# A chunked RWKV-7 scan on one core: small products of the two array halves issued in turn

## The chip, the core and the metric

The kernel runs on one core of a Trainium2 chip. The core has a matrix engine (PE, TensorE), which multiplies a stationary operand (`lhsT`, loaded by a weight load, PEld) with a moving operand (`rhs`) and writes to PSUM; a vector engine (DVE), a scalar engine (ACT) and GpSimd (POOL), which do the elementwise work; and SyncE (SP) and others, which issue DMAs. Each engine executes its own instructions in the order in which they stand. The metric is the device time of one execution in microseconds.

## The reference, cut to what matters

Two layers of a streaming encoder (256 tokens, width 2048, float32): attention and a feed-forward block, then RWKV-7 time mixing and a feed-forward block. The change is in the time mixing, a recurrence over tokens with a 64x64 state for each of 32 heads:

```
def step(state, inp):
    rt, wt, kt, vt, kkt, at = inp
    sa = einsum('bhvk,bhk->bhv', state, -kkt)
    state = state * wt + sa[..., None] * (kkt * at) + vt[..., None] * kt
    yt = einsum('bhvk,bhk->bhv', state, rt)
    return state, yt
_, y = lax.scan(step, state0, xs)          # then a norm per head, a gate, and out @ wo
```

## The kernel before

All large products split a float32 operand into a high and a low part and take three matmuls (L216 to L218, moving operand 512 wide; L236 to L238, 256 wide). I call these the large matmuls; DVE and ACT make their weight halves `whi` and `wlo` (L111, L112) from what the DMA queue of SP brings.

The scan does not step through tokens. Tokens go in 4 chunks of 64 and heads in 4 groups of 8 (`g`). Within a chunk the recurrence becomes small float32 products, each of them two passes of the matrix engine (a weight load and a matmul apiece), on a part of the 128x128 array: the rows by the partitions of the operands, the columns by the partitions of the output.

- `scan_operands` (L1110), for each of 8 panels: 16 products of 64x64, 8 on rows 0 to 63 and columns 0 to 63, then 8 on rows and columns 64 to 127, all into one PSUM bank (`ps_d`). This lies beside the projection `rwk`.
- `scan_pre` (L1169), for each group: for each of 8 heads 4 products of 64 rows by 128 columns; even heads use rows 0 to 63, odd heads rows 64 to 127. DVE masks each head's bank (L1172). In group 0 two heads go in one step (banks `ps_d` and `ps_c`), in the others one head (`ps_c`).
- `scan_chain`, for each group: the inverse of a triangular matrix is put together by 32x32 products (L1229, L1238, two halves of 16 each). Then chunk by chunk `c`: `within` (L1254, 8 products of 64x64) into `wps`; `carried` (L1265) adds 4 products with the state `SB` to it, and 4 more go to the output bank `yps` on the other half of the columns; ACT copies `wps` to `W` (L1270); 8 products with the inverse (L1281); ACT copies them to `VU` (L1283); the state's update (L1292, 2 x 4 products, one column half after the other), added to the decayed state by DVE (L1297, L1299); and the outputs (L1301, 8 products on column half `tb`). After every second chunk a head norm starts.

The chain is a generator that is advanced between the large matmuls of the projections `rwv` and `rwo` (`tick`); a scheduler in the framework then puts each engine's instructions in a fixed order, which differs somewhat from the order written. `ps(role)` takes PSUM banks in rotation: three for `mm`, two for `a`, one each for `b`, `c`, `d`.

Of the kernel before, what the change touches and what calls it, by code (L numbers as in the profile page):

```python
# [10 lines left out]
F32 = mybir.dt.float32  # L11
# [3 lines left out]
ALU = mybir.AluOpType  # L15
# [5 lines left out]
P = 128  # L21
# [13 lines left out]
class Kern:  # L35
# [1008 lines left out]
    def scan_operands(self, g, q, tmp, rq, kq):  # L1044

        nc, V_ = self.nc, self.vec
# [31 lines left out]
        for src, dst in ((sq, pn), (rk, pb)):  # L1078
            for t in range(2):
                for i in range(2):  # L1080
                    nc.tensor.matmul(dst[:, t, :], lhsT=src[:, i, t * P:(t + 1) * P], rhs=self.ind[:, i, :],
                                     start=i == 0, stop=i == 1)
# [20 lines left out]
        yield 4  # L1103

        ps = self.ps("d").rearrange("p (i c t) -> p i c t", i=2, c=4)
        for e in range(2):
            x = slice(64 * e, 64 * e + 64)
            for i in range(2):
                for c in range(4):
                    nc.tensor.matmul(ps[x, i, c, :], lhsT=kb[x, 2 * i + c // 2, 1 + c % 2, :], rhs=ar[x, 4 * i + c, 0, :],  # L1110
                                     start=True, stop=True)
        ms = tmp.tile([P, 8, 64], F32, name="ms", tag="ms")
# [31 lines left out]
    @staticmethod  # L1144
    def hx(h):

        return (h // 4) * 4 + (h % 2) * 2 + (h % 4) // 2

    def scan_pre(self, g, ld, sp):

        nc = self.nc
        KB, AR = [], []
        for q in range(2):
            kb = ld.tile([P, 4, 4, 64], F32, name="kb2", tag="KB", bufs=2)
            ar = ld.tile([P, 8, 2, 64], F32, name="ar2", tag="AR", bufs=4)
            (nc.scalar if g else nc.sync).dma_start(kb, self.kbd[2 * g + q])
            (nc.scalar if g else nc.sync).dma_start(ar, self.ard[2 * g + q])
            KB.append(kb.rearrange("p (i b) (e x) t -> p i (b e) (x t)", i=2, e=2))
            AR.append(ar.rearrange("p (i c) s t -> p i c s t", i=2))
            if g == 0:  # L1160
                yield 5 - q
        if g:
            yield 3
        QT = []
        for h in range(8):
            q, i, x = h // 4, (h % 4) // 2, slice(64 * (h % 2), 64 * (h % 2) + 64)
            ps = self.ps("c" if g or h % 2 else "d").rearrange("p (c x) -> p c x", c=4)
            for c in range(4):
                nc.tensor.matmul(ps[:, c, :], lhsT=KB[q][x, i, c, :], rhs=AR[q][x, i, c].rearrange("p s t -> p (s t)"),  # L1169
                                 start=True, stop=True)  # L1170
            qt = sp.tile([P, 4, 128], F32, name="qt", tag="QT", bufs=16)
            nc.vector.tensor_tensor(qt, ps, self.tri.unsqueeze(1).to_broadcast([P, 4, 128]), op=ALU.mult)  # L1172
            QT.append(qt)
            if g or h % 2:
                yield 0

        for q in range(2):
            x = KB[q].rearrange("p i c x -> p (i c) x")
            pl = self.PL[g][:, 2 * q:2 * q + 2, :].rearrange("p i c -> p (i c)")
            (nc.gpsimd if g > 1 else nc.vector).tensor_tensor(x, x, pl.unsqueeze(2).to_broadcast([P, 8, 128]), op=ALU.mult)  # L1180
        yield 0
        return KB, AR, QT

    def scan_chain(self, g, sp, pre, v, norm, done):
        nc, a = self.nc, self.a
        KB, AR, QT = pre

        aside = nc.gpsimd if g else nc.vector

        def bB(c):  # L1190
            return 64 * (1 - c % 2)

        def bK(c):
            return 64 * (c % 2)
# [4 lines left out]
        VU = sp.tile([P, 4, 512], F32, name="VU", tag="VU")  # L1199
        for par in range(2):  # L1200
            b = 64 * (1 - par)
# [3 lines left out]
            for blk in (1, 0):  # L1205
                dst = TP[b + 32 * blk:b + 32 * blk + 32].rearrange("s h a i -> s (h a) i")[:, :, 32 * blk:32 * blk + 32]
# [6 lines left out]
        for pr_ in range(4):  # L1213
            ps = self.ps("dc"[pr_ % 2])
# [7 lines left out]
        done.add(("kbt", g))  # L1222
        hx = self.hx
        ps1 = self.ps("mm").rearrange("p (h a i) -> p h a i", h=8, a=2)
        for par in range(2):
            b = 64 * (1 - par)
            for h in range(8):
                for ap_ in range(2):
                    nc.tensor.matmul(ps1[b + 32:b + 64, hx(h), ap_, :], lhsT=QT[h][b:b + 32, 2 * ap_ + par, 32:64],  # L1229
                                     rhs=T1[b:b + 32, hx(h), ap_, :], start=True, stop=True)  # L1230
            nc.scalar.copy(T1[b + 32:b + 64], ps1[b + 32:b + 64])
        yield 0
        ps2 = self.ps("mm").rearrange("p (h a i) -> p h a i", h=8, a=2)
        for par in range(2):
            b = 64 * (1 - par)
            for h in range(8):
                for ap_ in range(2):
                    nc.tensor.matmul(ps2[b:b + 32, h, ap_, :], lhsT=T1[b + 32:b + 64, h, ap_, :],  # L1238
                                     rhs=TP[b + 32:b + 64, h, ap_, 32:64], start=True, stop=True)
            nc.scalar.copy(TP[b:b + 32, :, :, 32:64], ps2[b:b + 32])  # L1240


        W = sp.tile([P, 512], F32, name="W", tag="W")

        SB = sp.tile([P, 4, 128], F32, name="SB", tag="SB")
        SD = sp.tile([P, 4, 64], F32, name="SD", tag="SD")
        nc.gpsimd.memset(SB, 0.0)
        wps, yps = {}, None

        def within(c):  # L1250

            wps[c] = self.ps("mm")[bB(c):bB(c) + 64, :]
            for h in range(8):
                nc.tensor.matmul(wps[c][:, h * 64:(h + 1) * 64], lhsT=QT[h][bK(c):bK(c) + 64, c, 0:64],  # L1254
                                 rhs=VU[bK(c):bK(c) + 64, c, h * 64:(h + 1) * 64], start=h == 0, stop=c == 0 and h == 7)

        within(0)
        for c in range(4):
            t, b, tb = c // 2, bB(c), 64 * (c % 2)
            if c % 2 == 0:  # L1260
                yps = self.ps("b")

            def carried(dst, s):
                for pr_ in range(4):
                    nc.tensor.matmul(dst[:, pr_ * P:(pr_ + 1) * P], lhsT=AR[pr_ // 2][:, pr_ % 2, c, s, :],  # L1265
                                     rhs=SB[:, pr_, :], start=s == 1 and pr_ == 0, stop=s == 0 and pr_ == 3)

            if c:
                carried(wps[c], 0)
            nc.scalar.copy(W[b:b + 64, :], wps[c])  # L1270
            if c:
                carried(yps[tb:tb + 64, :], 1)
                if c < 3:
                    for e in range(2):
                        x = slice(64 * e, 64 * e + 64)
                        aside.tensor_tensor(SD[x], SB[x, :, x], self.PL[g][x, :, c].unsqueeze(2).to_broadcast([64, 4, 64]),
                                            op=ALU.mult)
            yield 0
            pu = self.ps("mm")
            for h in range(8):  # L1280
                nc.tensor.matmul(pu[b:b + 64, h * 64:(h + 1) * 64], lhsT=TP[b:b + 64, hx(h), t, :],  # L1281
                                 rhs=W[b:b + 64, h * 64:(h + 1) * 64], start=True, stop=True)
            nc.scalar.copy(VU[b:b + 64, c, :], pu[b:b + 64, :])  # L1283
            if c < 3:
                within(c + 1)
            yield 0
            if c < 3:
                ps = self.ps("mm")[:, :256].rearrange("p (r x) -> p r x", r=4)
                for e in range(2):
                    x = slice(64 * e, 64 * e + 64)  # L1290
                    for pr_ in range(4):
                        nc.tensor.matmul(ps[x, pr_, :], lhsT=KBT[pr_][:, c, x],  # L1292
                                         rhs=VU[:, c, (2 * pr_ + e) * 64:(2 * pr_ + e + 1) * 64], start=True, stop=True)
                for e in range(2):
                    x = slice(64 * e, 64 * e + 64)
                    if c:
                        nc.vector.tensor_tensor(SB[x, :, x], ps[x], SD[x], op=ALU.add)  # L1297
                    else:
                        nc.vector.tensor_copy(SB[x, :, x], ps[x])  # L1299
            for h in range(8):  # L1300
                nc.tensor.matmul(yps[tb:tb + 64, h * 64:(h + 1) * 64], lhsT=QT[h][:, c, 64:128],  # L1301
                                 rhs=VU[:, c, h * 64:(h + 1) * 64], start=c == 0 and h == 0, stop=h == 7)
            if c % 2:
                norm(g, t, yps, v)
            yield 0

# [192 lines left out]
```

## Time and profile before

| | us |
|---|---|
| median of 3 runs | 2492.48 (2490.84 to 2494.36) |
| the profiled execution, its own time | 2493.24 |
| its span, first to last instruction | 2491.5 |

The small products of the scan lie between about 1320 and 1717 us of the span. In the listings a matmul's time runs from its start to its modelled end, and matmuls overlap, so the time that a burst costs is read from its first start to the first start of what follows.

### The profile page before, as it was taken

What the parts mean: (1) busy time and instruction counts of PE and PEld (TensorE: products, weight loads), DVE (VectorE), ACT (ScalarE), POOL (GpSimd) and SP (SyncE); (2) the same over time, 40 slices, a digit from 0 to 9 for tenths busy, and PEclk for the clock granted to TensorE, in tenths of its full rate; (3) what the DMA queues carried; (4) which work ended last, traced back from release to release, by engine and by line L of the source; (5) the groups of instructions that cost most, each with busy time, mean ns of one, the idle gap of its engine ahead of it and who ended that gap; (6) DMA issues with size and microseconds to landing.
All of it is one profiled execution on the core that took longest, in us unless ns stands there. A gap on an engine that the chain in (4) does not pass through costs nothing.

```text
span 2491.5 us, 42348 instructions
## 1 busy us (share of the span) xinstructions
PE 2437.7 (98%) x17128; PEld 2214.8 (89%) x17128; DVE 1595.8 (64%) x2498; ACT 1161.6 (47%) x1669; POOL 205.6 (8%) x234
## 2 busy tenths in 40 slices
PE   8999999999999999997999999999999999999997
PEld 8998889989989989986899988888998998998986
DVE  6667978645656646669478965557864555655655
ACT  5435646444444434455556544444544443443443
POOL 1000000000000000014301252211000000000001
PEclk9999999999999999998999999999999999999999
DMA  8665455555555555553456754324555555555554
GB/s 280 209 198 180 140 177 176 188 190 192 187 193 187 189 197 187 191 181 119 154 176 221 255 194 131 108 92 154 177 195 193 189 190 190 187 191 194 187 192 139
DMA packets 140852, 453.01 MB, mean 182 GB/s; under 512 B 27536, under 2 KB 27792, under 8 KB 140656
## 3 DMA queue, kind: packets, MB, share of 16 engines
q1 hardware_dynamic: 120176, 424.46, 51.4%
q0 software_dynamic: 5568, 16.52, 1.8%
q10 hardware_dynamic: 14912, 9.32, 1.2%
q8 instruction: 134, 2.20, 0.3%
q14 instruction: 62, 0.51, 0.1%
HBM read 433.99 MB, written 15.20 MB: 180 GB/s over the span
## 4 chain that ended last, share of the span: by engine, by line
PE 92%; DVE 4%; issue 1%; DMA 1%; ACT 1%; POOL 0%; SPq 0%; DVEq 0%; ACTq 0%
PE ps_mm L236 8%; PE ps_mm L237 7%; PE ps_mm L238 7%; PE ps_mm L218 7%; PE ps_mm L216 7%; PE ps_mm L217 7%; PE ps_a L216 7%; PE ps_a L217 6%; PE ps_a L218 6%; PE ps_a L238 6%; PE ps_a L236 6%; PE ps_a L237 6%; PE ps_c L1169 1%; DVE wlo L112 1%; PE ps_mm L1254 1%
## 5 line engine op out<-in xcount | busy, mean ns | idle before, releaser
L112 DVE TENSOR_TENSOR wlo<-raw,whi 128x1024 fp32r<-128x1024 f32 (+1 forms) x766 | 937.6, 1229 | 621.6 <-ACT whi L111 604.1
L111 ACT CAST whi<-raw 128x1024 fp32r<-128x1024 f32 (+1 forms) x776 | 809.7, 1047 | 681.1 <-PE ps_mm L218 221.0
L236 PE MATMUL ps_mm<-fxh,whi 128*128 128x256 f32 x1024 | 287.7, 281 | 0.0
L237 PE MATMUL ps_mm<-fxl,whi 128*128 128x256 f32 x1024 | 287.3, 281 | 0.0
L236 PE MATMUL ps_a<-fxh,whi 128*128 128x256 f32 x1024 | 286.9, 280 | 0.0
L237 PE MATMUL ps_a<-fxl,whi 128*128 128x256 f32 x1024 | 286.9, 280 | 0.0
L238 PE MATMUL ps_a<-fxh,wlo 128*128 128x256 f32 x1024 | 286.9, 280 | 0.0
L238 PE MATMUL ps_mm<-fxh,wlo 128*128 128x256 f32 x1024 | 286.9, 280 | 0.0
L217 PE MATMUL ps_mm<-wlo,uh 128*128 128x512 f32 (+1 forms) x544 | 208.2, 383 | 0.0
L216 PE MATMUL ps_mm<-whi,uh 128*128 128x512 f32 (+1 forms) x544 | 208.2, 383 | 0.0
L218 PE MATMUL ps_mm<-whi,ul 128*128 128x512 f32 (+1 forms) x544 | 208.2, 383 | 0.0
L217 PE MATMUL ps_a<-wlo,uh 128*128 128x512 f32 (+1 forms) x512 | 196.0, 383 | 0.0
L238 PEld LDWEIGHTS ps_a<-fxh,wlo 128*128 128x128 f32 x1024 | 195.9, 191 | 0.0
L238 PEld LDWEIGHTS ps_mm<-fxh,wlo 128*128 128x128 f32 x1024 | 195.9, 191 | 0.0
L218 PE MATMUL ps_a<-whi,ul 128*128 128x512 f32 (+1 forms) x512 | 195.7, 382 | 0.0
L216 PE MATMUL ps_a<-whi,uh 128*128 128x512 f32 (+1 forms) x512 | 195.5, 382 | 0.0
L236 PEld LDWEIGHTS ps_mm<-fxh,whi 128*128 128x128 f32 x1024 | 192.2, 188 | 0.6 <-DVE r L630 0.2
L237 PEld LDWEIGHTS ps_mm<-fxl,whi 128*128 128x128 f32 x1024 | 192.3, 188 | 0.3
L237 PEld LDWEIGHTS ps_a<-fxl,whi 128*128 128x128 f32 x1024 | 192.2, 188 | 0.0
L236 PEld LDWEIGHTS ps_a<-fxh,whi 128*128 128x128 f32 x1024 | 192.2, 188 | 0.0
L632 ACT CAST uh<-r 128x256 fp32r<-128x256 f32 x128 | 51.9, 406 | 271.1 <-DVE r L631 271.1
L237 PE MATMUL ps_mm<-ml,whi 128*128 128x256 f32 x416 | 118.0, 284 | 6.7 <-DVE ml L807 6.7
(404 smaller groups left out, 4796.5 us busy)
## 6 DMA issues: line engine op xcount, KB each, us to landing
raw<-in_ffn SPq DMA_DIRECT2D x512, 512.0 KB, 4.3
raw<-in_wk SPq DMA_DIRECT2D x32, 512.0 KB, 4.6
raw<-in_wv SPq DMA_DIRECT2D x32, 512.0 KB, 4.1
raw<-in_wo SPq DMA_DIRECT2D x32, 512.0 KB, 4.1
raw<-in_rwr SPq DMA_DIRECT2D x32, 512.0 KB, 4.6
raw<-in_rwk SPq DMA_DIRECT2D x32, 512.0 KB, 4.3
raw<-in_rwv SPq DMA_DIRECT2D x32, 512.0 KB, 5.1
raw<-in_rwo SPq DMA_DIRECT2D x32, 512.0 KB, 4.3
```

Source lines behind the costliest of these rows:

```text
L111: self.nc.scalar.copy(hi[:, x], src[:, x])
L112: (eng or self.nc.vector).tensor_tensor(lo[:, x], src[:, x], hi[:, x].bitcast(F32), op=ALU.subtract)
L216: nc.tensor.matmul(ps[t][:, x], lhsT=xh, rhs=wh[:, k, :], start=st, stop=False)
L217: nc.tensor.matmul(ps[t][:, x], lhsT=xh, rhs=wl[:, k, :], start=False, stop=False)
L218: e = nc.tensor.matmul(ps[t][:, x], lhsT=xl, rhs=wh[:, k, :], start=False, stop=sp)
L236: nc.tensor.matmul(ps[m], lhsT=wh[:, k, cl], rhs=xh, start=first and k == 0, stop=False)
L237: nc.tensor.matmul(ps[m], lhsT=wh[:, k, cl], rhs=xl, start=False, stop=False)
L238: e = nc.tensor.matmul(ps[m], lhsT=wl[:, k, cl], rhs=xh, start=False, stop=last and k == 3)
L632: nc.scalar.copy(UH[-1][:, m % 4, :], r)
L1169: nc.tensor.matmul(ps[:, c, :], lhsT=KB[q][x, i, c, :], rhs=AR[q][x, i, c].rearrange("p s t -> p (s t)"), start=True, stop=True)
L1254: nc.tensor.matmul(wps[c][:, h * 64:(h + 1) * 64], lhsT=QT[h][bK(c):bK(c) + 64, c, 0:64], rhs=VU[bK(c):bK(c) + 64, c, h * 64:(h + 1) * 64] ...
```

## The change

Small products that stand on different halves of the array's rows or columns are issued alternately, not half by half. `scan_operands` alternates its two halves. `scan_pre` takes the heads in pairs in all groups (one bank `ps_d`, one `ps_c`), alternates them, and masks both at the end; a group has four such steps, each of two ticks where there were eight of one. The 32x32 products alternate, and both copies follow at the end. `within` makes two chunks at once (0 and 1 ahead of the loop, 2 and 3 in chunk 1), `carried` alternates its two targets, the state's update alternates its halves, and the outputs of two chunks are made together in the odd chunk. The number of products is the same.

```diff
@@ scan_operands
-        for e in range(2):
-            for i in range(2):
-                for c in range(4):
+        for i in range(2):
+            for c in range(4):
+                for e in range(2):
                     nc.tensor.matmul(ps[x, i, c, :], ...
@@ scan_pre
-        for h in range(8):
-            ps = self.ps("c" if g or h % 2 else "d")...
+        for pr_ in range(4):
+            ps = [self.ps(r)... for r in "dc"]
             for c in range(4):
+                for e in range(2):
+                    nc.tensor.matmul(ps[e][:, c, :], lhsT=KB[q][x, i, c, :], ...
+            for e in range(2):
+                nc.vector.tensor_tensor(qt, ps[e], self.tri..., op=ALU.mult)
+            yield 1 if g else 0
@@ scan_chain, both sets of 32x32 products
-        for par in range(2):
-            for h in range(8):
-                for ap_ in range(2):
+        for h in range(8):
+            for ap_ in range(2):
+                for par, b in ((0, 64), (1, 0)):
                     nc.tensor.matmul(ps1[b + 32:b + 64, hx(h), ap_, :], ...
+        for b in (64, 0):
             nc.scalar.copy(T1[b + 32:b + 64], ps1[b + 32:b + 64])
@@ scan_chain, within
+        def within(c0):
+            ps = self.ps("mm")
             for h in range(8):
+                for c in (c0, c0 + 1):
+                    nc.tensor.matmul(ps[bB(c):bB(c) + 64, x], lhsT=QT[h][bK(c):bK(c) + 64, c, 0:64], ...
@@ scan_chain, the loop over chunks
-            if c:
-                carried(wps[c], 0)
-            nc.scalar.copy(W[b:b + 64, :], wps[c])
-            if c:
-                carried(yps[tb:tb + 64, :], 1)
+            if c:
+                for pr_ in range(4):
+                    for s, dst in ((0, wps[b:b + 64, :]), (1, yps[tb:tb + 64, :])):
+                        nc.tensor.matmul(dst[:, pr_ * P:(pr_ + 1) * P], lhsT=AR[pr_ // 2][:, pr_ % 2, c, s, :], ...
+            nc.scalar.copy(W[b:b + 64, :], wps[b:b + 64, :])
...
-            if c < 3:
-                within(c + 1)
+            if c == 1:
+                wps = within(2)
             yield 0
             if c < 3:
-                for e in range(2):
-                    for pr_ in range(4):
+                for pr_ in range(4):
+                    for e in range(2):
                         nc.tensor.matmul(ps[x, pr_, :], lhsT=KBT[pr_][:, c, x], ...
...
-            for h in range(8):
-                nc.tensor.matmul(yps[tb:tb + 64, ...], lhsT=QT[h][:, c, 64:128], ...
             if c % 2:
+                for h in range(8):
+                    for d in (c - 1, c):
+                        nc.tensor.matmul(yps[db:db + 64, ...], lhsT=QT[h][:, d, 64:128], ...
                 norm(g, t, yps, v)
```

In the changed kernel the small products have these lines: L1110 stays; L1169 is L1172; L1229 is L1231; L1238 is L1240; L1254 is L1259; L1265 is L1272; L1281 is L1283; L1292 is L1295; L1301 is L1308.

Three places in the order of PE's instructions. The first is chunk 0 of group 0, from the products with the inverse to the state's update. Before:

```order
L218 MATMUL ps_a<-whi,ml 128x512
L1281 MATMUL ps_mm<-W,TP 64x64 x8
L1254 MATMUL ps_mm<-VU,qt 64x64 x8
L1292 MATMUL ps_mm<-VU,kbt 64x64 x8
L1301 MATMUL ps_b<-VU,qt 64x64 x8
L216 MATMUL ps_a<-whi,mh 128x512
```

and in the changed kernel:

```order
L1283 MATMUL ps_mm<-W,TP 64x64 x8
L218 MATMUL ps_a<-whi,ml 128x512
L216 MATMUL ps_a<-whi,mh 128x512
L217 MATMUL ps_a<-wlo,mh 128x512
L218 MATMUL ps_a<-whi,ml 128x512
L216 MATMUL ps_a<-whi,mh 128x512
L1295 MATMUL ps_mm<-VU,kbt 64x64 x8
```

Between the inverse and the update, which needs ACT's copy to `VU`, five large matmuls stand where `within` stood, and no outputs follow the update.

The second is PE at the first product with the state (chunk 1 of group 0; `ar_15045` and `ar_15131` are the two panels of the group). Before:

```order
L218 MATMUL ps_a<-whi,ml 128x512
L1265 MATMUL ps_mm<-SB,ar_15045 64x128 x2
L1265 MATMUL ps_mm<-SB,ar_15131 64x128 x2
L1265 MATMUL ps_b<-SB,ar_15045 64x128 x2
L1265 MATMUL ps_b<-SB,ar_15131 64x128 x2
L216 MATMUL ps_a<-whi,mh 128x512
```

and in the changed kernel:

```order
L218 MATMUL ps_a<-whi,ml 128x512
L1272 MATMUL ps_mm<-SB,ar_15045 64x128
L1272 MATMUL ps_b<-SB,ar_15045 64x128
L1272 MATMUL ps_mm<-SB,ar_15045 64x128
L1272 MATMUL ps_b<-SB,ar_15045 64x128
L1272 MATMUL ps_mm<-SB,ar_15131 64x128
```

The two targets, which lie on different column halves, now take turns. In 2 of the 12 such places the scheduler still puts four of one ahead of four of the other.

The third is PE a little later in the same chunk, where group 1's preparation (`kb_15418`) meets the chain. Before:

```order
L218 MATMUL ps_a<-whi,ml 128x512
L1169 MATMUL ps_c<-ar_15419,kb_15418 128x128 x4
L1281 MATMUL ps_mm<-W,TP 64x64 x8
L1254 MATMUL ps_mm<-VU,qt 64x64 x8
L216 MATMUL ps_a<-whi,mh 128x512
```

and in the changed kernel, from the last two pairs of a step of two heads on:

```order
L1172 MATMUL ps_d<-ar_15419,kb_15418 128x128
L1172 MATMUL ps_c<-ar_15419,kb_15418 128x128
L1172 MATMUL ps_d<-ar_15419,kb_15418 128x128
L1172 MATMUL ps_c<-ar_15419,kb_15418 128x128
L1283 MATMUL ps_mm<-W,TP 64x64 x8
L1259 MATMUL ps_mm<-VU,qt 64x64 x16
```

One step holds two heads, and `within` makes two chunks. Of the 16 pairs of heads, 12 alternate throughout as here, three begin with two or three products of one head, and one has its halves apart.

## Rows read from the trace of the kernel before

**Rows 1.** The page: PE's busy time, and the engines of the chain that ended last.

```profile
PE 2437.7 (98%) x17128; PEld 2214.8 (89%) x17128; DVE 1595.8 (64%) x2498; ACT 1161.6 (47%) x1669; POOL 205.6 (8%) x234
...
PE 92%; DVE 4%; issue 1%; DMA 1%; ACT 1%; POOL 0%; SPq 0%; DVEq 0%; ACTq 0%
```

**Rows 2.** Busy time by stretch; after POOL: granted clock, DMA share, GB/s.

```profile
1320.00:1441.00 121.00, 121.00 (x1048) 114.07 (x1047) 107.60 (x245) 66.77 (x116) 26.69 (x46) 1.00 0.71 242
...
1580.00:1654.00 74.00, 73.65 (x704) 60.74 (x703) 39.78 (x72) 35.19 (x57) 15.21 (x15) 1.00 0.37 116
1654.00:1717.00 63.00, 62.81 (x600) 51.58 (x600) 34.20 (x66) 30.12 (x48) 5.83 (x6) 0.95 0.25 80
```

**Rows 3.** Timeline of PE, chunk 0 of group 0: start, us, then xcount passes.

```profile
1481.55 0.97 PE L1281 MATMUL ps_mm<-W,TP 64*64 64x64 f32 x13
1482.30 0.27 PE L1254 MATMUL ps_mm<-VU,qt 64*64 64x64 f32 x1
1482.35 0.22 PE L1281 MATMUL ps_mm<-W,TP 64*64 64x64 f32 x1
...
1483.37 0.79 PE L1292 MATMUL ps_mm<-VU,kbt 128*64 128x64 f32 x13
...
1485.02 0.50 PE L216 MATMUL ps_a<-whi,mh 128*128 128x512 f32 x1
...
1485.91 0.76 PE L1265 MATMUL ps_mm<-SB,ar 128*64 128x128 f32 x5
1486.41 0.32 PE L1265 MATMUL ps_b<-SB,ar 128*64 128x128 f32 x1
1486.51 0.27 PE L1265 MATMUL ps_mm<-SB,ar 128*64 128x128 f32 x1
```

**Rows 4.** Timeline of PE: one panel of `scan_operands`, and one pair of heads.

```profile
1320.79 1.90 PE L1110 MATMUL ps_d<-ar,kb 64*64 64x64 f32 x32
1322.61 0.38 PE L236 MATMUL ps_mm<-mh,whi 128*128 128x256 f32 x1
...
1450.63 0.82 PE L1169 MATMUL ps_d<-ar,kb 64*128 64x128 f32 x5
1451.19 0.37 PE L1169 MATMUL ps_c<-ar,kb 64*128 64x128 f32 x1
...
1452.27 0.50 PE L216 MATMUL ps_a<-whi,mh 128*128 128x512 f32 x1
```

**Rows 5.** Timeline of PE: half of a 32x32 set, `within` alone, and what follows.

```profile
1474.38 1.19 PE L1238 MATMUL ps_mm<-TP,T 32*32 32x32 f32 x32
1475.50 1.14 PE L1254 MATMUL ps_mm<-VU,qt 64*64 64x64 f32 x16
1476.57 0.50 PE L216 MATMUL ps_a<-whi,mh 128*128 128x512 f32 x1
```

**Rows 6.** Timeline of PE: one head alone, an update with outputs, one target alone.

```profile
1489.02 1.16 PE L1169 MATMUL ps_c<-ar,kb 64*128 64x128 f32 x8
1490.10 0.97 PE L1281 MATMUL ps_mm<-W,TP 64*64 64x64 f32 x13
...
1494.60 0.97 PE L1292 MATMUL ps_mm<-VU,kbt 128*64 128x64 f32 x16
...
1496.43 0.50 PE L216 MATMUL ps_a<-whi,mh 128*128 128x512 f32 x1
...
1499.10 1.09 PE L1265 MATMUL ps_mm<-SB,ar 128*64 128x128 f32 x8
1500.12 0.50 PE L216 MATMUL ps_a<-whi,mh 128*128 128x512 f32 x1
```

**Rows 7.** ACT's and DVE's instructions by line: ns minimum, median, maximum.

```profile
L1270 ACT COPY W<-ps_mm x16: 578/580/583, 1480.2 to 1705.0; 64x512 f32<-64x512 f32 x16
...
L1283 ACT COPY VU<-ps_mm x16: 578/580/583, 1482.7 to 1708.1; 64x512 f32<-64x512 f32 x16
...
L1297 DVE TENSOR_TENSOR SB<-ps_mm,SD x16: 406/422/430, 1495.6 to 1702.2; 64x256 f32<-64x256 f32 x16
```

More of the change, by code (lines that the diff above doesn't have):

```diff
@@ L1105, in scan_operands @@
         ps = self.ps("d").rearrange("p (i c t) -> p i c t", i=2, c=4)
-        for e in range(2):
-            x = slice(64 * e, 64 * e + 64)
-            for i in range(2):
-                for c in range(4):
+        for i in range(2):
+            for c in range(4):
+                for e in range(2):
+                    x = slice(64 * e, 64 * e + 64)
                     nc.tensor.matmul(ps[x, i, c, :], lhsT=kb[x, 2 * i + c // 2, 1 + c % 2, :], rhs=ar[x, 4 * i + c, 0, :],
@@ L1164, in scan_pre @@
         QT = []
-        for h in range(8):
-            q, i, x = h // 4, (h % 4) // 2, slice(64 * (h % 2), 64 * (h % 2) + 64)
-            ps = self.ps("c" if g or h % 2 else "d").rearrange("p (c x) -> p c x", c=4)
+        for pr_ in range(4):
+            q, i = pr_ // 2, pr_ % 2
+            ps = [self.ps(r).rearrange("p (c x) -> p c x", c=4) for r in "dc"]
             for c in range(4):
[L1169 to L1175, printed above, removed]
+                for e in range(2):
+                    x = slice(64 * e, 64 * e + 64)
+                    nc.tensor.matmul(ps[e][:, c, :], lhsT=KB[q][x, i, c, :],
+                                     rhs=AR[q][x, i, c].rearrange("p s t -> p (s t)"), start=True, stop=True)
+            for e in range(2):
+                qt = sp.tile([P, 4, 128], F32, name="qt", tag="QT", bufs=16)
+                nc.vector.tensor_tensor(qt, ps[e], self.tri.unsqueeze(1).to_broadcast([P, 4, 128]), op=ALU.mult)
+                QT.append(qt)
+            yield 1 if g else 0
         for q in range(2):
@@ L1224, in scan_chain @@
         ps1 = self.ps("mm").rearrange("p (h a i) -> p h a i", h=8, a=2)
-        for par in range(2):
-            b = 64 * (1 - par)
-            for h in range(8):
-                for ap_ in range(2):
+        for h in range(8):
+            for ap_ in range(2):
+                for par, b in ((0, 64), (1, 0)):
                     nc.tensor.matmul(ps1[b + 32:b + 64, hx(h), ap_, :], lhsT=QT[h][b:b + 32, 2 * ap_ + par, 32:64],
                                      rhs=T1[b:b + 32, hx(h), ap_, :], start=True, stop=True)
+        for b in (64, 0):
             nc.scalar.copy(T1[b + 32:b + 64], ps1[b + 32:b + 64])
@@ L1233, in scan_chain @@
         ps2 = self.ps("mm").rearrange("p (h a i) -> p h a i", h=8, a=2)
-        for par in range(2):
-            b = 64 * (1 - par)
-            for h in range(8):
-                for ap_ in range(2):
+        for h in range(8):
+            for ap_ in range(2):
+                for b in (64, 0):
                     nc.tensor.matmul(ps2[b:b + 32, h, ap_, :], lhsT=T1[b + 32:b + 64, h, ap_, :],
                                      rhs=TP[b + 32:b + 64, h, ap_, 32:64], start=True, stop=True)
+        for b in (64, 0):
             nc.scalar.copy(TP[b:b + 32, :, :, 32:64], ps2[b:b + 32])
@@ L1247, in scan_chain @@
         nc.gpsimd.memset(SB, 0.0)
-        wps, yps = {}, None
-        def within(c):
-            wps[c] = self.ps("mm")[bB(c):bB(c) + 64, :]
+        wps, yps = None, None
+        def within(c0):
+            ps = self.ps("mm")
             for h in range(8):
-                nc.tensor.matmul(wps[c][:, h * 64:(h + 1) * 64], lhsT=QT[h][bK(c):bK(c) + 64, c, 0:64],
-                                 rhs=VU[bK(c):bK(c) + 64, c, h * 64:(h + 1) * 64], start=h == 0, stop=c == 0 and h == 7)
-        within(0)
+                for c in (c0, c0 + 1):
+                    x = slice(h * 64, (h + 1) * 64)
+                    nc.tensor.matmul(ps[bB(c):bB(c) + 64, x], lhsT=QT[h][bK(c):bK(c) + 64, c, 0:64],
+                                     rhs=VU[bK(c):bK(c) + 64, c, x], start=h == 0, stop=c == 0 and h == 7)
+            return ps
+        wps = within(0)
         for c in range(4):
@@ L1261, in scan_chain @@
                 yps = self.ps("b")
-            def carried(dst, s):
+            if c:
                 for pr_ in range(4):
-                    nc.tensor.matmul(dst[:, pr_ * P:(pr_ + 1) * P], lhsT=AR[pr_ // 2][:, pr_ % 2, c, s, :],
-                                     rhs=SB[:, pr_, :], start=s == 1 and pr_ == 0, stop=s == 0 and pr_ == 3)
-            if c:
-                carried(wps[c], 0)
-            nc.scalar.copy(W[b:b + 64, :], wps[c])
-            if c:
-                carried(yps[tb:tb + 64, :], 1)
-                if c < 3:
-                    for e in range(2):
-                        x = slice(64 * e, 64 * e + 64)
-                        aside.tensor_tensor(SD[x], SB[x, :, x], self.PL[g][x, :, c].unsqueeze(2).to_broadcast([64, 4, 64]),
-                                            op=ALU.mult)
+                    for s, dst in ((0, wps[b:b + 64, :]), (1, yps[tb:tb + 64, :])):
+                        nc.tensor.matmul(dst[:, pr_ * P:(pr_ + 1) * P], lhsT=AR[pr_ // 2][:, pr_ % 2, c, s, :],
+                                         rhs=SB[:, pr_, :], start=s == 1 and pr_ == 0, stop=s == 0 and pr_ == 3)
+            nc.scalar.copy(W[b:b + 64, :], wps[b:b + 64, :])
+            if 0 < c < 3:
+                for e in range(2):
+                    x = slice(64 * e, 64 * e + 64)
+                    aside.tensor_tensor(SD[x], SB[x, :, x], self.PL[g][x, :, c].unsqueeze(2).to_broadcast([64, 4, 64]),
+                                        op=ALU.mult)
             yield 0
@@ L1284, in scan_chain @@
             if c < 3:
-                within(c + 1)
+                ps = self.ps("mm")[:, :256].rearrange("p (r x) -> p r x", r=4)
+            if c == 1:
+                wps = within(2)
             yield 0
             if c < 3:
-                ps = self.ps("mm")[:, :256].rearrange("p (r x) -> p r x", r=4)
-                for e in range(2):
-                    x = slice(64 * e, 64 * e + 64)
-                    for pr_ in range(4):
+                for pr_ in range(4):
+                    for e in range(2):
+                        x = slice(64 * e, 64 * e + 64)
                         nc.tensor.matmul(ps[x, pr_, :], lhsT=KBT[pr_][:, c, x],
@@ L1299, in scan_chain @@
                         nc.vector.tensor_copy(SB[x, :, x], ps[x])
-            for h in range(8):
-                nc.tensor.matmul(yps[tb:tb + 64, h * 64:(h + 1) * 64], lhsT=QT[h][:, c, 64:128],
-                                 rhs=VU[:, c, h * 64:(h + 1) * 64], start=c == 0 and h == 0, stop=h == 7)
             if c % 2:
+                for h in range(8):
+                    for d in (c - 1, c):
+                        db = 64 * (d % 2)
+                        nc.tensor.matmul(yps[db:db + 64, h * 64:(h + 1) * 64], lhsT=QT[h][:, d, 64:128],
+                                         rhs=VU[:, d, h * 64:(h + 1) * 64], start=d == 0 and h == 0, stop=h == 7)
                 norm(g, t, yps, v)
```

## Prediction

> **What bounds the kernel now.** First the page: PE is busy 98% of the span and makes up 92% of the chain that ended last [rows 1]. Then the stretches in which the small products lie: in all three PE is busy over 99% of the time, next to DVE at 89% (1320 to 1441), 54% (1580 to 1654) and 54% (1654 to 1717) [rows 2]. So between 1320 and 1717 us a microsecond that PE no longer needs comes off the end, unless a wait takes its place. No stretch is short of DMA (share 0.71, then 0.37 and 0.25).
>
> What a small product costs PE is read from starts in the timeline. `within` alone is 16 passes of 64x64 in 1476.57 - 1475.50 = 1.07 us [rows 5]. A row of 16 such passes lasts 1.14 us and one of 13 lasts 0.97 [rows 3, 5], so a pass comes every 0.17/3 = 57 ns; 16 x 0.057 = 0.91 us, and the other 0.16 us is the change of shape to the next burst. The 32-wide half set has 32 passes in 1.12 us [rows 5].
>
> The row that decides is the seam between two bursts. After 13 of the 16 passes of L1281 the first pass of L1254 starts, 1482.30, and only then the last three of L1281 [rows 3]. L1281 writes columns 64 to 127 here, L1254 columns 0 to 63. L1265 does it too: after five of eight passes to `ps_mm` the first to `ps_b` starts at 1486.41, and the next to `ps_mm` follows at 1486.51. So two halves of the array do work at the same time, and in program order PE looks only about three passes ahead. The row halves do the same: the odd head's first pass starts at 1451.19, 0.56 us after the even head's and 1.08 us before the large matmuls return [rows 4].
>
> **The change, part by part.** I take it that with the halves issued in turn both streams run at the pace of one throughout, so that a pair costs what one half costs alone.
>
> - L1110: a panel is 1322.61 - 1320.79 = 1.82 us [rows 4]; one half alone is 16 passes of 64x64, 1.07 [rows 5]. 8 x 0.75 = 6.0 us.
> - Heads: one alone is 1490.10 - 1489.02 = 1.08 us [rows 6]. In group 0 a pair is 1452.27 - 1450.63 = 1.64 [rows 4] and becomes 1.08; two of the four pairs start with three products of one head and get less than half of that: 2 x 0.56 + 2 x 0.23 = 1.6. In groups 1 to 3, 24 heads alone become 12 pairs; one pair stays apart and one starts unevenly, so about 10.75 x 1.08 = 11.6. Together 13.2 us.
> - 32x32 products: 16 half sets become 8 pairs. The ends are that nothing is won (0) and that a whole half set of 1.0 us without its change of shape goes (8.0). A weight load and a matmul every 35 ns is the densest issue that any row shows, 17.5 ns an instruction [rows 5]; two streams need half of that, which no row shows over more than three passes. I take the middle, 4.0 us.
> - `within`: a group has now one alone (1.07), three behind L1281, each 1483.37 - 1481.55 = 1.82 [rows 3], and a last L1281 alone (1.07, the same shape): 7.6 us. After: one for chunks 0 and 1 (1.07), three L1281 alone (3.21), and one L1281 with the next pair (1.82): 6.1. 4 x 1.5 = 6.0 us.
> - `carried`: the second target starts 1486.41 - 1485.91 = 0.50 us after the first [rows 3], and one target alone is 1.02 [rows 6]. So 8 joined bursts are 1.52 and 4 with the targets apart 2.04, 20.3 us; after, ten at 1.02 and the two that stay apart, 14.3. That is 6.0 us.
> - Update and outputs: 1485.02 - 1483.37 = 1.65 in chunks 0 and 2 [rows 3], 1496.43 - 1494.60 = 1.83 in chunk 1 [rows 6], and outputs alone (1.07, the same pace) in chunk 3: 6.2 us a group. After: three updates of 8 passes a half, each 1.07 - 8 x 0.057 = 0.61, and two outputs of 1.07: 4.0. 4 x 2.23 = 8.9 us.
>
> Sum: 6.0 + 13.2 + 4.0 + 6.0 + 6.0 + 8.9 = 44.1 us.
>
> What is given back. Three covers get thinner. The copy to `VU` (580 ns [rows 7]) had `within` (0.93 us of starts) in front of the update and now mostly has five or six large matmuls; three take 1485.91 - 1485.02 = 0.89 us with their changes of shape [rows 3], so five take some 1.3: covered, as long as ACT isn't in a weight cast. The copy to `W` starts after both targets, not after the first, and has six large matmuls or a pair of heads (1.1 us or more) behind it. The two additions to `SB` (422 ns each [rows 7]) lose the outputs as a cover in even chunks and have five or more large matmuls. The copies of the 32x32 halves come two in a row now, with six or more large matmuls behind them. What is queued behind a late copy on PE is everything, since PE keeps its order; each cover has room for a few tenths of a microsecond, so I expect a wait at a few of the 16 chunks only. DVE at 89% beside L1110 may take back part of the 6.0 us there: what PE saves must come with `wlo` sooner. For both I take 3 us; the ends are 0 and 10. The tick counts don't change, so no step comes later in the projections.
>
> The profiled execution took 2493.24 us: 2493.2 - 44.1 + 3 = 2452.1. Its time is 0.8 us above the median of the runs, so the forecast is 2451 us, 1.7% less. 0.2% (5 us) is about what a measurement of this kernel can tell from no change.
>
> **A rule that speaks against it.** L1110's panel is 32 passes in 1.82 us where 32 x 0.057 + 0.16 is 1.98 [rows 4, 5]: about three passes are hidden at its seam, too, though both halves write the same bank `ps_d`. The Trainium skill (TensorEngine Tiling (Array Packing), Restrictions and Gotchas) says that different row tiles cannot access the same PSUM bank simultaneously; by that rule L1110, the 32x32 products and `within`, whose halves share a bank, would win nothing, and the sum would be 28.1. By that rule the trace disagrees, for three passes. It also says (TensorE: Matmul & The Clock Gate, Part 3) that weight loads overlap with matmuls in flight only when the row group differs; by that, `carried`, updates and outputs, which differ in columns alone, would win nothing. The trace disagrees there as well, in the rows of L1265.
>
> **Rivals.**
>
> 1. Halves that share a bank take turns over a longer run, though they overlap for three passes. The 6.0, 4.0 and 6.0 us are lost: 2451 + 16 = 2467 us. For it: no row shows more than three passes. Against it: at the seam of L1110 nothing slows.
> 2. PE can't issue faster than the densest row, 17.5 ns an instruction. Then 32x32 wins nothing (4.0 us less) and a pass of 64x64 comes every 35 ns in place of 28.5: a full pair burst takes 32 x 0.035 + 0.16 = 1.28 instead of 1.07, 24 of them (L1110, `within`, outputs) 5.0 us, and 12 updates half of that each, 1.3. 2451 + 10 = 2461 us. For it: the look-ahead is short. Against it: the pace goes with the columns (35 ns a pass at 32, 1.07/16 = 67 at 64, 1.08/8 = 135 at 128 [rows 5, 6]), so it is set by the array and not by issue.
> 3. Halves of different columns alone take turns: `carried`, updates and outputs lose 15 us, 2466. Against it are the rows of L1265.
> 4. The other side: a turn from half to half empties the array, as a change of shape does (0.16 us [rows 3, 5]). L1110, heads, `within` and outputs have 128 products each, 32x32 256, `carried` and updates 96 each: some 960 turns. At 0.16 us that is 154 us, and with none of the 44 us won, about 2493 + 154 = 2647 us. It decides from 44/960 = 46 ns a turn. Against it: at the seams the starts take turns with no such hole, 1482.30 and 1482.35, 1486.41 and 1486.51 [rows 3].
> 5. The covers fail: at each of 16 chunks `W`, `VU` and `SB` in the open, 0.58 + 0.58 + 0.84 us and some 0.2 us of signalling each, 2.6 us, give 42 us back: 2493 us, no change. For it: the scheduler fixed the order and may have counted the small products as longer than they become. Against it: five or more large matmuls stand at nearly every such place.
>
> **How the numbers follow.** The forecast 0.68, rival 1 0.10, rival 2 0.10, rival 3 0.04, rival 4 0.03, rival 5 0.03, and 0.02 for something else that loses. The low end is the forecast with all of the 32x32 half sets won (4 us), no wait (3 us) and without the half-speed clock that stands now in 1654 to 1717 (0.95 of 63 us, so 3 us lost [rows 2]): 2451 - 10 = 2441. The high end takes in rivals 1 to 3 and 3 us more of waits: 2470. Range 2441 to 2470. Faster by over 0.2%: 0.68 + 0.10 + 0.10 + 0.04 = 0.92; within it 0.03; slower 0.05, rivals 4 and the unnamed.
>
> **What would show it.** In the timeline after, L1110's panels at about 1.1 us instead of 1.82, with starts in pairs a few ns apart; a pair of heads at 1.1; L1231 and L1240 sets of 64 passes at 1.1 (all won) to 2.2 (nothing won); L1308 with 32 passes in 1.1; L1272 at 1.0. The large matmuls keep their pace. PE's waits for `W`, `VU` and `SB` stay under 5 us in all. The span shrinks in 1320 to 1717 alone, by some 41 us, with the stages before and behind unchanged. The prediction is wrong if pairs cost more than one half alone (rivals 1 to 4, told apart by which lines do), or if they do not and idle time of PE appears ahead of L1283, L1295 or L1272 (rival 5).

## The result and the profile after

The changed kernel takes 2448.38 us (median of 4 runs, 2442.61 to 2452.91) against 2491.66 for the kernel before on the same chip (4 runs, 2484.75 to 2494.36): ratio 0.9831, 95% interval 0.9811 to 0.9851. That is 43 us, or 1.7%, faster. The forecast was 2451. The profiled execution took 2452.91 us.

On the page of the changed kernel PE is busy 43.8 us less for the same number of instructions [rows 1]:

```profile
PE 2393.9 (98%) x17128; PEld 2172.4 (89%) x17128; DVE 1594.6 (65%) x2498; ACT 1159.3 (47%) x1669; POOL 212.0 (9%) x234
```

Its timeline of PE at the places of [rows 3 to 6], columns as there:

```profile
1320.34 1.15 PE L1110 MATMUL ps_d<-ar,kb 64*64 64x64 f32 x32
1321.42 0.38 PE L236 MATMUL ps_mm<-mh,whi 128*128 128x256 f32 x1
...
1325.41 0.28 PE L236 MATMUL ps_mm<-mh,whi 128*128 128x256 f32 x1
...
1444.86 0.37 PE L1172 MATMUL ps_d<-ar,kb 64*128 64x128 f32 x1
1444.86 0.37 PE L1172 MATMUL ps_c<-ar,kb 64*128 64x128 f32 x1
...
1445.95 0.50 PE L216 MATMUL ps_a<-whi,mh 128*128 128x512 f32 x1
...
1476.70 0.32 PE L1272 MATMUL ps_mm<-SB,ar 128*64 128x128 f32 x1
1476.71 0.32 PE L1272 MATMUL ps_b<-SB,ar 128*64 128x128 f32 x1
...
1477.73 0.50 PE L216 MATMUL ps_a<-whi,mh 128*128 128x512 f32 x1
...
1483.83 0.69 PE L1295 MATMUL ps_mm<-VU,kbt 128*64 128x64 f32 x16
1484.34 1.10 PE L1308 MATMUL ps_b<-VU,qt 128*64 128x64 f32 x32
1485.38 0.50 PE L216 MATMUL ps_a<-whi,mh 128*128 128x512 f32 x1
...
1635.50 1.19 PE L1240 MATMUL ps_mm<-TP,T 32*32 32x32 f32 x62
1636.62 0.50 PE L217 MATMUL ps_a<-wlo,roh 128*128 128x512 f32 x1
```

Starts come in pairs 0 to 10 ns apart, and a pair costs what one half cost alone. A panel takes 1321.42 - 1320.34 = 1.08 us (1.82 before), two heads 1.09 (1.64), the product with the state to both targets 1.03 (1.52 where joined before), the outputs of two chunks 1.04. A whole 32x32 set of 64 passes (two records are missing) takes 1.12 us, as long as half a set did [rows 5].

Where the time came from, for each term of the sum: all its bursts, from each one's first start to the first start of what follows, added up over the trace (the differences are of unrounded sums).

| us | before | after | won | predicted |
|---|---|---|---|---|
| L1110 | 14.6 | 8.6 | 6.0 | 6.0 |
| heads | 33.2 | 20.3 | 12.8 | 13.2 |
| 32x32 | 18.3 | 11.2 | 7.1 | 4.0 |
| `within` and inverse | 31.1 | 25.0 | 6.1 | 6.0 |
| `carried` | 20.1 | 15.8 | 4.4 | 6.0 |
| update and outputs | 24.8 | 16.1 | 8.7 | 8.9 |
| sum | | | 45.0 | 44.1 |

Below, the *scan* is the stretch from the first start of a head product to the last start of an output. The trace's summary of these two lines in the changed kernel (in ns the shortest, median and longest, then the first and last start):

```profile
L1172 PE MATMUL ps_d<-ar,kb x128: 271/272/374, 1444.9 to 1613.0; 64*128 64x128 f32 x128
...
L1308 PE MATMUL ps_b<-VU,qt x256: 221/222/271, 1484.3 to 1667.2; 128*64 128x64 f32 x128
```

It lasts 1667.2 - 1444.9 = 222.3 us. In the kernel before, L1169 starts at 1450.6 and L1301 ends its starts at 1710.5: 259.9. The stretch of L1110, from its first to its last start, went from 114.5 to 109.2 us. So 37.6 + 5.3 = 42.9 us went in these two. The profiled time fell by only 40.3, since the part behind the scan was 2.9 us longer in this execution; over the traces of all kernels that part, which none of them changes, goes from 780.7 to 784.3 us, and the start of L1110 from 1314 to 1324. That is why single executions of kernels are compared below by their scans.

Busy time by stretch (PE, PEld, DVE, ACT, POOL, then granted clock, DMA share, GB/s), and what PE waited for in the scan (total, times, longest):

```profile
1320.00:1435.00 115.00, 115.00 (x1043) 108.14 (x1042) 106.39 (x241) 65.47 (x115) 26.68 (x46) 1.00 0.73 252
...
1435.00:1509.00 74.00, 70.59 (x738) 56.05 (x737) 48.69 (x80) 30.30 (x41) 47.93 (x70) 1.00 0.51 161
...
1617.00:1675.00 58.00, 57.41 (x617) 45.84 (x618) 36.45 (x72) 30.85 (x48) 5.91 (x6) 1.00 0.32 101
```

```profile
PE ps_mm L1272 <- DVE SB L1300: 2.4, 2, 1.7
PE ps_mm L1231 <- DMA T<-tnd: 1.1, 2, 0.7
PE ps_b L1272 <- DVE YN L1344: 0.6, 1, 0.6
PE ps_d L1172 <- DVE qt L1176: 0.4, 1, 0.4
```

`T` is the operand of the first 32x32 products, which a DMA brings; `YN` belongs to the head norm, and `qt` is a masked head. PE has no hole beside L1110, though DVE is now at 106.4 of 115 us, 93% (89% before, [rows 2]). Yet the 33 large matmuls behind a panel now take 1325.41 - 1321.42 = 3.99 us; in the kernel before the same 33 took 3.87, 1322.61 [rows 4] to 1326.48. Most of them start every 118 ns in place of 113. It is so at the five panels that have 256-wide products behind them, and not at the three with 512-wide ones. Added up, the large matmuls beside L1110 cost 0.7 us more.

In the scan PE's idle time rose from 1.1 to 5.7 us: that is what was given back. Against it, the half-speed stretch of the kernel before is not in this execution, whose clock is 1.00 in all these stretches where [rows 2] has 0.95.

### The profile page after: what moved, and what is told of

Its sections match the earlier page's. It is cut to its first block, busy times and chain, and to the rows that moved or that the text cites. A ratio compares the mean times of both kernels' runs of the same rounds, so it can differ in the third digit from the quotient of the medians.

```text
span 2451.1 us, 42351 instructions
## 1 busy us (share of the span) xinstructions
PE 2393.9 (98%) x17128; PEld 2172.4 (89%) x17128; DVE 1594.6 (65%) x2498; ACT 1159.3 (47%) x1669; POOL 212.0 (9%) x234
```

## Experiments

The kernel before ran beside each group on the same chip; its medians were 2492.92, 2492.97 and 2487.4 us.

**Turns or joining.** The change does two things: it joins products into longer bursts, and issues the halves of a burst in turn. The first kernel has the change's bursts, but each half by half. This is one of its eight loops; the others are turned round alike (cut):

```diff
-            for c in range(4):
-                for e in range(2):
+            for e in range(2):
+                for c in range(4):
                     nc.tensor.matmul(ps[e][:, c, :], ...
```

> The changed kernel with every turn undone: the same pairs of heads, the same joined bursts of two chunks and the same copies at the end, but each burst issued half by half. If the turns are what wins, a pair of heads costs 1.64 us as in group 0 before (16 pairs, 26 us in place of 20.3 after and 33.2 before), a panel of L1110 1.82 again, an update 0.9, and only the fewer changes of shape and the seams are won: 8 to 14 us below the kernel before, about 2481 us. If instead fewer and longer bursts or the new order won the time, it stays with the changed kernel: 2448 us, and the bursts are short here as well.

The second is the kernel before with turns in the bursts that it has already (L1110, 32x32, `carried`, update); heads, `within` and outputs stay apart.

> The kernel before with turns only inside the bursts that it has: L1110, the 32x32 products (their copies at the end), the two targets of the state product, and the update's halves. Heads, the products within a chunk and the outputs stay as they were. If turns win by themselves, the sum is 6.0 (L1110) + 7 (32x32) + 5 (targets) + 3.4 (updates, 12 x 0.29) - 1.4 for seams that are lost = 20 us: 2472 us. If the joining of bursts is needed, or if turns cost something at each turn, it is at 2490 us or above.

Measured: 2480.66 us (ratio 0.9955, 0.9937 to 0.9973) and 2471.48 us (0.992, 0.9902 to 0.9938). So joining alone is worth 12 us, turns alone 21, and the other 10 of the change's 43 need both, since a head alone has no other to take turns with. By the intervals the first two are good to some 5 us, and the 10 is less sure. The stretch of L1110 and the scan together say the same in the traces: 10.4 us for joining, 20.5 for turns, 42.8 for both. In the first kernel's timeline a pair of heads takes 1482.90 - 1481.26 = 1.64 us, as in [rows 4]; the only gain is the seam, where five of one are issued ahead of the first of the other:

```profile
1481.26 0.82 PE L1172 MATMUL ps_d<-ar,kb 64*128 64x128 f32 x5
1481.81 0.37 PE L1172 MATMUL ps_c<-ar,kb 64*128 64x128 f32 x1
...
1482.90 0.27 PE L1283 MATMUL ps_mm<-W,TP 64*64 64x64 f32 x1
```

**How fine the turns must be.** L1110's four panels of each pair of groups take turns of 1, 2, 4 and 8 products:

```diff
+        run = (1, 2, 4, 8)[(2 * g + q) % 4]
+        for n in range(0, 8, run):
+            for e in range(2):
+                for m in range(n, n + run):
```

> The changed kernel with L1110's turns of 1, 2, 4 and 8 products (each two passes) in panels 0 and 4, 1 and 5, 2 and 6, 3 and 7. If PE looks some three passes ahead of a busy half, turns of 2 products are as good as of 1 (1.08 us a panel), turns of 4 lose the start of the second half alone (four passes of 0.058 us: 1.31 us), and turns of 8 are the kernel before (1.82 us). If only a strict alternation overlaps, turns of 2 already cost 1.4 us or more. The total moves by 2 us at most.

```profile
1332.94 1.20 PE L1112 MATMUL ps_d<-ar,kb 64*64 64x64 f32 x32
1334.07 0.38 PE L236 MATMUL ps_mm<-mh,whi 128*128 128x256 f32 x1
...
1337.93 0.28 PE L236 MATMUL ps_mm<-mh,whi 128*128 128x256 f32 x1
...
1349.06 1.54 PE L1112 MATMUL ps_d<-ar,kb 64*64 64x64 f32 x32
1350.53 0.39 PE L236 MATMUL ps_mm<-mh,whi 128*128 128x256 f32 x1
...
1365.53 1.90 PE L1112 MATMUL ps_d<-ar,kb 64*64 64x64 f32 x32
1367.36 0.38 PE L236 MATMUL ps_mm<-mh,whi 128*128 128x256 f32 x1
```

These are turns of 2, 4 and 8: 1.13, 1.47 and 1.83 us; turns of 1 took 1.08. A turn of two products (four passes) costs almost nothing, and from four on most of a turn is in the open. That fits a look-ahead of about three passes; turns of 4 came out 0.16 us above what I expected. The total was 2449.89 us (one execution).

The same trace shows what slows the large matmuls behind a panel. Behind turns of 1 the 33 take 3.99 us, as in the changed kernel; behind turns of 2, 4 and 8 they take 3.87 (1337.93 - 1334.07 = 3.86 above), as in the kernel before. So turns of two products cost 0.05 us more in the panel and save 0.12 behind it, and are the better choice there. Why the finest turns slow what follows stays open.

**More than two parts.** L1110 on all four 64x64 parts, the products of one half of `i` going to the other column half and to bank `ps_c`:

```diff
+                    y = 64 * ((e + i) % 2)
+                    nc.tensor.matmul(ps[i][y:y + 64, c, :], ...
-        nc.scalar.copy(ms, ps...)
+        for i in range(2):
+            nc.scalar.copy(ms[:, 4 * i:4 * i + 4, :], ps[i])
```

> The changed kernel with L1110 on all four 64x64 parts of the array in turn: products of i = 1 go to the other column half and to another bank, so that parts that share columns write different banks; eight DMAs bring a panel's result where four did. If the four parts work independently, a panel is 8 passes deep: about 0.62 us in place of 1.08. If parts that share rows or columns take turns, or if PE can't issue an instruction every 7.3 ns, it stays near 1.08 us. The total moves by 4 us at most.

The panel is as quick as expected, 1380.16 - 1379.54 = 0.62 us (first timeline), yet the kernel took 2454.24 us in its one execution, and its L1110 stretch 110.1 us, no less than with the change. Its scan took 226.2 us, 3.8 more, with a wait of 2.2 us for the DMA of `T`, one of 1.3 us for a mask, and a stretch at the lower clock behind them (0.58 in 1460 to 1464 us). Beside L1110 the gain is lost at once (windows):

```profile
1379.54 0.27 PE L1111 MATMUL ps_d<-ar,kb 64*64 64x64 f32 x2
1379.55 0.27 PE L1111 MATMUL ps_c<-ar,kb 64*64 64x64 f32 x2
...
1380.16 0.38 PE L236 MATMUL ps_mm<-mh,whi 128*128 128x256 f32 x1
...
1388.69 1.84 PE L1081 MATMUL ps_b<-rcst,rk 128*128 128x4 f32 x8 [0.99 <-DVE rk L1070]
```

```profile
1384.00:1388.00 4.00, 3.46 (x30) 3.20 (x28) 4.00 (x6) 2.09 (x2) 2.66 (x5) 1.00 0.39 103
1388.00:1392.00 4.00, 3.31 (x15) 3.23 (x16) 3.93 (x9) 0.17 (x1) 0.00 (x0) 0.62 0.59 189
1392.00:1396.00 4.00, 4.00 (x22) 4.00 (x21) 4.00 (x13) 0.94 (x3) 1.11 (x2) 0.53 0.67 217
```

DVE is busy 4.00 of 4 us and PE waits for it (0.99 us at L1081). Right behind that hole the granted clock is 0.62 and 0.53: the lower level, for 6.8 us. What PE saved beside L1110 came out as waits for DVE and lost clock.

The same for the 32x32 products, on four parts:

```diff
+                for half in range(2):
+                    for par, b in ((0, 64), (1, 0)):
+                        k, o = h + 4 * half, b + 32 - 32 * half
+                        nc.tensor.matmul(ps1[o:o + 32, hx(k), ap_, :], ...
```

> The changed kernel with the 32x32 products on four parts in turn (heads 4 to 7 on the neighbouring 32 columns; four copies of half the width bring the results to their places where two did). Two streams took 64 passes in about 1.0 us. If the parts stay independent and PE can issue that fast (an instruction every 4 ns), a set takes 0.55 to 0.65 us with its change of shape. If issue is the limit, it stays between that and 1.1 us, and the pace in the middle of a burst is PE's issue floor. The total moves by 4 us at most.

```profile
1581.40 0.70 PE L1246 MATMUL ps_mm<-TP,T 32*32 32x32 f32 x58 [0.89 <-ACT T L1238]
1582.03 1.15 PE L1267 MATMUL ps_mm<-VU,qt 64*64 64x64 f32 x32
...
1629.78 0.75 PE L1233 MATMUL ps_mm<-T,qt 32*32 32x32 f32 x64
1630.46 0.50 PE L216 MATMUL ps_a<-whi,roh 128*128 128x512 f32 x1
```

A set takes 0.68 us (1630.46 - 1629.78) where the change's takes 1.12. But the copies are four small ones now, and one set waits 0.89 us for ACT. The scan stayed at 222.1 us, the total at 2453.16 (one execution).

In chunk 1 the products with the inverse and `within` for chunks 2 and 3 can share a burst of three streams (`also` is the inverse's product of one head):

```diff
+            if c == 1:
+                wps = within(2, inv)
...
             for h in range(8):
+                also(h)
                 for c in (c0, c0 + 1):
```

> The changed kernel with three streams in chunk 1: each of the 8 products with the inverse is followed by a product of chunk 2 and one of chunk 3 (three different 64x64 parts, of which one shares its rows and one its columns with the first). If parts that share only rows or only columns work at once, the burst of 48 passes takes what 16 take alone, 1.07 us in place of 1.82, in 4 groups 3.0 us: 2445 us. If sharing rows or columns makes them take turns, the burst stays near 1.8 us and the time at 2448 us. The total can hardly tell these apart, the burst can.

```profile
1534.74 0.27 PE L1285 MATMUL ps_mm<-W,TP 64*64 64x64 f32 x1
1534.75 0.27 PE L1260 MATMUL ps_mm<-VU,qt 64*64 64x64 f32 x2
...
1535.66 0.22 PE L1285 MATMUL ps_mm<-W,TP 64*64 64x64 f32 x1
```

The 48 passes make 16 rounds, one every (1535.66 - 1534.74) / 15 = 61 ns, close to the pace of one stream (57). The scan is 219.8 us, 2.5 shorter, about as expected. The total, 2450.73 us (2441.34 to 2451.27; ratio 0.9823, 0.9802 to 0.9844), can't be told from the change's.

**What PE waits for now.** The longest wait left is that of the product with the state for `SB`. PE and, in the second fence, DVE of the changed kernel:

```profile
1488.06 0.43 PE L1272 MATMUL ps_mm<-SB,ar 128*64 128x128 f32 x2
1489.10 0.29 PE L1272 MATMUL ps_b<-SB,ar 128*64 128x128 f32 x1 [0.61 <-DVE YN L1344]
...
1500.57 0.32 PE L1272 MATMUL ps_mm<-SB,ar 128*64 128x128 f32 x1 [1.74 <-DVE SB L1300]
```

```profile
1496.63 1.21 DVE L112 TENSOR_TENSOR wlo<-raw,whi 128x1024 fp32r<-128x1024 f32 x1
...
1498.15 0.68 DVE L1176 TENSOR_TENSOR qt<-ps_d,tri 128x512 f32<-128x512 f32 x1
...
1498.83 0.68 DVE L1176 TENSOR_TENSOR qt<-ps_c,tri 128x512 f32<-128x512 f32 x1
...
1499.50 0.41 DVE L1300 TENSOR_TENSOR SB<-ps_mm,SD 64x256 f32<-64x256 f32 x1
...
1500.09 0.43 DVE L1300 TENSOR_TENSOR SB<-ps_mm,SD 64x256 f32<-64x256 f32 x1
```

The additions stand behind a split and two masks that now come together. I put the wait down to the masks and parted them by a tick:

```diff
-            yield 1 if g else 0
+                if g or e:
+                    yield 0
```

> The changed kernel with a tick between the two masks of a pair of heads in groups 1 to 3, as before the change. If the wait of 1.7 us ahead of a state product came from the two masks that stand one behind the other on DVE ahead of the state's addition, PE's waits for that addition fall from 2.4 us to under 1 us. If they came from the norm's and the weights' instructions in the same queue, they stay. The total moves by 2 us at most.

The wait stayed, 2.5 us in two waits, so that theory fell. The waits for the masks themselves and for `T` vanished, that for the output bank grew from 0.6 to 1.1 us, and the scan took 219.5 us (2447.44 us, one execution). Next, the head norm's steps, cut so that they leave DVE free:

```diff
+        if t == 0:
+            yield 3
...
-        yield 6
+        yield 6 if t else 2
```

> The changed kernel with the first head norm of a group cut in two: its variance and the small steps of its root wait three ticks, until the state's addition of the next chunk has been issued; the ticks are taken off the pause behind it. If the addition to SB is late because the norm's chain of small steps stands ahead of it on DVE, PE's waits for SB fall from 2.4 us to under 0.8 and the scan takes 220.5 us. If the weight splits (1.2 us each) are what it stands behind, the waits stay at 2 us or more.

```profile
PE ps_mm L1231 <- DMA T<-tnd: 2.6, 2, 2.5
PE ps_mm L1272 <- DVE SB L1300: 1.5, 2, 0.9
```

The wait fell from 2.4 to 1.5 us, not as far as expected, and one for `T` grew to 2.5 us. So the norm is a part of it; which of DVE's other steps holds the rest stays open. The scan took 223.8 us, with the granted clock at 0.58 in 1456 to 1460 us, right behind that wait; the total was 2445.72 (one execution).

**Together.** All of four parts (both), three streams and parted masks:

> The changed kernel with everything above: L1110 and the 32x32 products on four parts, three streams in chunk 1, the masks apart. If each gain adds up: 8 x 0.45 + 4 + 3.0 + 2 = 12.6 us below the changed kernel, 2436 us. If the stretch of L1110 is held by DVE, which is busy some 92% there after the change, its 3.6 us are lost; if the waits on DVE, ACT and DMA grow as the products shrink, half of the rest goes too: 2443 us.

2451.27 us (2443.96 to 2454.92; 0.9825, 0.9807 to 0.9844): nothing beyond the change. Its windows have the same picture as that of four parts alone:

```profile
1388.00:1392.00 4.00, 2.79 (x24) 2.73 (x24) 4.00 (x6) 1.87 (x2) 1.54 (x3) 1.00 0.44 115
1392.00:1396.00 4.00, 3.71 (x17) 3.63 (x18) 3.93 (x9) 0.17 (x1) 0.00 (x0) 0.58 0.48 170
```

So I left the four parts out, and ran the rest beside the changed kernel itself, on one chip: three streams with parted masks, the same with the cut norm, and the change again.

> The changed kernel with three streams in chunk 1 and the masks of a pair a tick apart, without the four-part products. In single looks the scan took 222.4 us after the change, 219.8 with three streams and 219.5 with the masks apart. If both hold and add, 5 us less than the changed kernel beside it: 2443 us. If the two were chance or win the same idle time, it is within 2 us of it.

> The changed kernel with three streams, masks apart and the norm later. If the three add, 6 to 7 us less than the changed kernel beside it, about 2441 us, and an interval below it. If the later norm only moves the wait to the group norm's transposes, it equals the run with three streams and masks apart.

> The changed kernel itself, as a control on the same chip: 2448 us, 1.7 to 1.8% under the kernel before. Nothing else is expected of it.

| | us | ratio to before, 95% |
|---|---|---|
| three streams, parted masks | 2444.59 (2442.28 to 2445.35) | 0.9817 (0.9795 to 0.984) |
| and the cut norm | 2447.08 (2442.25 to 2451.41) | 0.9827 (0.9805 to 0.9849) |
| the change again | 2448.85 (2446.68 to 2454.88) | 0.9846 (0.9822 to 0.987) |

The first lies 4.3 us under the change and their runs don't overlap, but the intervals of the ratios do: it points to a further gain of a few microseconds and doesn't show it.

## Why the prediction was right

**What bounds.** PE did: what it no longer needed between 1320 and 1717 us came off the end, 42.9 us of stage time for 45.0 of bursts. Of the 2.1 between them 0.7 went beside L1110, to the slower large matmuls behind its panels; "The large matmuls keep their pace", a sign that the prediction gave, didn't hold there. Idle time outside the bursts grew by 2.8 us in the scan (the other 1.8 of the 4.6 stand in the bursts of the table), and the other products of the scan took 1.3 us less. The half-speed stretch of before, some 3 us (0.05 x 63 us, [rows 2]), is spread over both: it lies in that 1.3 and in the table's column of before.

**One pair costs what one half costs.** This held for row halves (heads), column halves (`carried`, outputs) and diagonal halves in one bank (L1110, 32x32, `within`), and with the bursts put back half by half some 31 of the 43 us went. Four terms of the sum are within 0.4 us.

**Two terms were mis-sized.** "I take the middle, 4.0 us" for the 32x32 products was too low: 7.1, near the upper end of 8.0. I had no row with a denser issue than 17.5 ns an instruction and let that weigh; in the change a set of 64 passes, 128 instructions, takes 1.12 us with its change of shape, under 9 ns each. (Some 0.7 of the 7.1 is the half-speed stretch of before: one half set in it took 1.84 us.) `carried` was too high, 4.4 in place of 6.0. Eight of the ten joined bursts take 1.02 us as forecast; two, both of chunk 2, take 2.03 and 1.49. Their second target is the output bank, which the norm of the two chunks before still reads (L1344, until 1488.96 and 1600.08 us); the first passes to it start at 1489.10 and 1600.22. In the kernel before, and with turns alone, the second target stood apart in all four places of chunk 2 and came behind that read. In two of these places the order of the changed kernel brings it forward to the first target, and my sum costed that at nothing. The two errors nearly cancel, and that is luck.

**Given back: 3 us predicted, 4.6 measured** as idle time of PE in the scan (5.7 - 1.1). `SB` was named as a cover that gets thin, and it is the largest (2.4); the waits for the bank, `T` and the masks were not named. `W` and `VU` stayed covered. PE shows no wait for DVE beside L1110 yet; with panels of 0.62 us it does. The half-speed stretch of before is gone, as the low end of the range allowed. But in the profile of the change run again the granted clock is 0.62 in 1456 to 1460 us, inside the scan, right behind a wait of 1.1 us for the DMA of `T`, so its absence is no effect of the change that I can show.

**The rivals.** Rival 1 (one bank) fell by L1110's 1.08 us, rival 2 (issue) by the 32x32 sets, rival 3 (columns) by L1272 and L1308, rival 4 (a hole at each turn) by all pairs, rival 5 (covers) by the sum of the waits. Both rules of the Trainium skill that spoke against the change are not borne out for these products. By the Trainium skill (TensorEngine Tiling (Array Packing), Restrictions and Gotchas), different row tiles can't access one PSUM bank at the same time. The trace disagrees, over whole bursts, with panels at 1.08 us. The row halves here write different partitions of the bank; row halves that write the same partitions of one bank weren't tried, so what the rule says stays open for those. By the Trainium skill (TensorE: Matmul & The Clock Gate, Part 3), weight loads overlap with matmuls in flight only where row groups differ. The trace disagrees there too: column halves alone, on the same rows, overlap as fully, 1.03 us in L1272.

## What to carry to other kernels

Small products that use part of the array cost PE here as much as one part's stream if streams on different parts are issued in turns of one or two products (two was the better beside L1110). So look in the order of the instructions for runs of more than that on one part. Then look at once for what the saved time was hiding: the banks that are now held longer, and the engine that is next. With the next engine at 93%, a further gain on PE turned into waits here, and with them came lost clock.

## What the runs showed of the hardware

- PE doesn't start its passes strictly in the order in which they stand: it takes those of another part of the array some three passes ahead (half by half, five passes of one head start before the first of the other, and its last three behind that). So halves overlap over a whole burst only if they are issued in turn.
- Four parts of the array work at once: a panel of 32 passes of 64x64 in 0.62 us against 1.08 with two and 1.82 half by half.
- PE's issue goes below what I had taken for near its limit: 64 passes (128 instructions) of 32x32 in 0.68 us, and less the 0.16 us for the change of shape that is, as an estimate, 4 ns an instruction.
- The 256-wide matmuls behind a panel of L1110 in turns of one product keep a slower pace: 33 of them take 3.99 us, and 3.87 behind turns of two or more.
- The granted clock fell to its lower level behind waits of PE for DVE (PE busy 3.31 to 3.46 of 4 us, then 0.53) and for the DMA of `T` (1.54 of 4 us, then 0.58, with the norm cut), but in the kernel before also behind 8 us with no wait over 0.2 us (PE busy 3.81 and 4.00 of 4 us, then 0.50 from 1672 us). It didn't fall behind the 1.74 us wait at 1500 us of the change, whose stretch has 1.00. What decides between them stays open.
